# Regrouping the small matmuls of a chunked recurrence and of attention scores on TensorE

## The chip, the core and the metric

The program runs on one core of a Trainium2 chip. The metric is device time in microseconds (us) for one execution, as the median of the runs shown. TensorE has two clock levels, 1.2 and 2.4 GHz; the profile shows which share of the full level was granted in a stretch.

## What is computed

One decoder block on 512 tokens of width 1024, all in fp32. The parts that matter here are the RWKV-7 recurrence (12 heads of 64) and the scores of the dilated attention (12 heads of 64 in three groups):

```python
def step(state, inp):
    r_t, w_t, k_t, v_t, kk_t, a_t = inp
    sa = -jnp.einsum('bhvk,bhk->bhv', state, kk_t)
    state = (state * w_t[:, :, None, :]
             + sa[..., None] * (kk_t * a_t)[:, :, None, :]
             + v_t[..., None] * k_t[:, :, None, :])
    y = jnp.einsum('bhvk,bhk->bhv', state, r_t)
    return state, y
...
s = jnp.einsum('bhrnqd,bhrnkd->bhrnqk', qb, kc, preferred_element_type=jnp.float32)
s = s * (HEAD_DIM ** -0.5)
```

Around them stand the input projection (1024 to 6912 columns), the output projections and a SwiGLU of width 2816.

## The kernel before, in words

Every large product is made of three fp32r matmuls (high by high, high by low, low by high), each 128x128 by 128x512. Those of the input projection carry the names hh, hl, hi and lo; this text calls one of them a **filler**, since the scheduler sets them between the small matmuls. A small fp32 matmul leaves two records in the trace, here called **passes**.

The recurrence is cut into 8 chunks of 64 tokens (`c`), and runs for two groups of three head pairs: `rwkv_group(0)` and `rwkv_group(1)`. A pair is two heads, `e` = 0 and 1, that lie on partitions 0 to 63 and 64 to 127. In each group, after vectors are prepared (lines 413 to 512) and a forward substitution runs on VectorE (lines 515 to 530), come:

- the **block inverses** (lines 539 to 557): for each pair, 16 products `T` (`ps<-T,Sg`, 32 by 32, line 543) into one bank, copies of the result into `Q` by both engines, 16 products `Q` (`ps<-N,Q`, line 554) into one bank, and copies into `N`. In both, the 8 chunks of one head come first, then those of the other.
- the **chunk loop** (lines 565 to 619). Each chunk has a chain: six products `px` (`ps<-UV,Sg`, line 571), a scaling on ScalarE into `xs` (line 573), six products with `N` (`ps<-xs,N`, line 578), copies to `UV` on both engines (line 580), six products `h` (`ps<-UV,BK`, line 587), two VectorE operations on `H` (lines 593 and 594), and copies of `H` to `UV` (lines 595 and 596), which the next chunk reads.
- the **output products** (lines 598 to 609), after each odd chunk, for it and the chunk ahead of it. For each head one bank `py` is filled: a product with the state (`ps<-H,AR`, 64 by 64 of the array, line 607; none for chunk 0) and one with `UV` (`ps<-UV,Sg`, 128 by 64 of the array, line 608) by turns, pair after pair. ScalarE then copies the bank to `yb`. In a group these are 42 products of the first kind and 48 of the second.

The attention scores (lines 705 to 731) are made head by head: for each of four heads, 12 products `ps<-k,q` on 64 partitions, 128 or 256 columns wide, then a masked scaling and maxima on VectorE.

The order on each engine is set by a list scheduler that keeps dependencies, with priorities: `rwkv_group` runs under `tc.high_priority(PRI)`, so fillers of the sequences in `SEQ` are set where the chain would leave TensorE empty. PSUM has banks under four tags: three `mm`, two `b`, two `c`, one `y`. The program's order is fixed when it is built; nothing is reordered by the program at run time.

Of the kernel before, what the change touches and what calls it, by code (L numbers as in the profile page):

```python
# [18 lines left out]
P = 128  # L19
D = 1024  # L20
S = 512
KT = D // P
NTT = S // P
HD = 64
NPAIR = 6
GP = 3
NCH = 8
C = 64
# [25 lines left out]
A_M0 = 0  # L54
# [30 lines left out]
def block_kernel(ctx, tc, x, vec, cst, cst2, cst3, crow, ada, win0, lora, wts, wa, out):  # L85
    nc = tc.nc
    V, A, G = nc.vector, nc.scalar, nc.gpsimd
# [19 lines left out]
    def mm(o, l, r, start, stop):  # L107
        return nc.tensor.matmul(o, l, r, start=start, stop=stop)  # L108
# [159 lines left out]
    with ExitStack() as ph0:  # L268
# [83 lines left out]
        t = tmp("tg", 3)[:, 0:S]  # L352
# [7 lines left out]
        t = tmp("tg", 3)[:, 0:S]  # L360
# [37 lines left out]
    def rwkv_group(gi):  # L398
# [139 lines left out]
            G.memset(N[64 * e + 32:64 * e + 64, 0:32, :], 0.0)  # L538
        for p in range(GP):
            pq = bank("c")  # L540
            for e in range(2):
                for c in range(NCH):
                    mm(pq[64 * e + 32:64 * e + 64, c * 32:(c + 1) * 32], Sg[p][0:32, e, c, 32:64], t1a[:, e, :, p * NCH + c], True, True)
            qs = rp.tile([P, NCH * 32], F32, tag="xs", name=nm("Q"), bufs=2).rearrange("p (c t) -> p c t", t=32)
            pqv = pq[:, 0:256].rearrange("p (c t) -> p c t", c=NCH)
            A.copy(qs[32:64], pqv[32:64])
            V.tensor_copy(qs[96:128], pqv[96:128])
            for e in range(2):
                (A.copy, V.tensor_copy)[XE[e]](Sg[p][0:64, e, :, 0:C], AR[p][64 * e:64 * e + 64, :, 0:C])
            pn = bank("c")  # L550
            for e in range(2):
                hi32 = slice(64 * e + 32, 64 * e + 64)
                for c in range(NCH):
                    mm(pn[64 * e:64 * e + 32, c * 32:(c + 1) * 32], qs[hi32, c, :], N[hi32, 32:64, p * NCH + c], True, True)
            pnv = pn[:, 0:256].rearrange("p (c t) -> p c t", c=NCH)
            A.copy(N[0:32, 32:64, p * NCH:(p + 1) * NCH], pnv[0:32].rearrange("p c t -> p t c"))
            V.tensor_copy(N[64:96, 32:64, p * NCH:(p + 1) * NCH], pnv[64:96].rearrange("p c t -> p t c"))


        yb = rp.tile([P, GP, NTT, 2, HD], F32, tag="yb", name=nm("yb"))  # L560
# [4 lines left out]
        for c in range(NCH):  # L565
            px = bank("c")
            pxv = px[:, 0:GP * HD].rearrange("p (a v) -> p a v", a=GP)
            for p in range(GP):
                for e in range(2):
                    rows = slice(64 * e, 64 * e + 64)  # L570
                    mm(pxv[rows, p, :], Sg[p][:, e, c, 0:C], UV[:, c, e, p, :], True, True)
            xs = rp.tile([P, NCH * 32], F32, tag="xs", name=nm("xs"), bufs=2)[:, 0:GP * HD].rearrange("p (a v) -> p a v", a=GP)
            A.activation(xs, pxv, AF.Copy, scale=-1.0)
            pus = [bank("c"), bank("c")]
            for p in range(GP):
                for e in range(2):
                    rows = slice(64 * e, 64 * e + 64)
                    last_mm[0] = mm(pus[e][rows, p * HD:(p + 1) * HD], N[rows, :, p * NCH + c], xs[rows, p, :], True, True)
            for e in range(2):
                (V.tensor_copy if e else A.copy)(UV[0:64, c, e, :, :], pus[e][64 * e:64 * e + 64, 0:GP * HD].rearrange("p (a v) -> p a v", a=GP))  # L580
            if c < NCH - 1:
                ph = bank("c")
                phv = ph[:, 0:GP * HD].rearrange("p (a v) -> p a v", a=GP)
                for p in range(GP):
                    for e in range(2):
                        rows = slice(64 * e, 64 * e + 64)
                        mm(phv[rows, p, :], BN[p][:, c, rows], UV[:, c, e, p, :], True, True)
                Hn = rp.tile([P, GP, HD], F32, tag="H", name=nm("H"), bufs=3)
                db = dg[:, c, :, None].to_broadcast([P, GP, HD])
                if c == 0:  # L590
                    V.tensor_tensor(out=Hn, in0=phv, in1=db, op=ALU.mult)
                else:
                    V.tensor_tensor(out=Hn, in0=H, in1=phv, op=ALU.add)
                    V.tensor_tensor(out=Hn, in0=Hn, in1=db, op=ALU.mult)
                V.tensor_copy(UV[0:64, c + 1, 0], Hn[0:64])
                A.copy(UV[0:64, c + 1, 1], Hn[64:128])
            Hs.append(H)
            if c % 2 == 1:
                for e in range(2):
                    rows = slice(64 * e, 64 * e + 64)  # L600
# [8 lines left out]
                    A.copy(yb[:, :, c // 2, e, :], py[:, 0:GP * HD].rearrange("p (a v) -> p a v", a=GP))  # L609
# [95 lines left out]
    Ss = []  # L705
    for j in range(4):
        hp, e = j // 2, j % 2
        rows = slice(64 * e, 64 * e + 64)
        sb = ap_.tile([P, 1920], F32, tag="S", name=nm("S"), bufs=4)
        Ss.append(sb)  # L710
        q, k = qT[0][hp][rows], kT[0][hp][rows]
        b0, b1 = bank("b"), bank("c")
        mm(b0[:, 0:128], q[:, 0:128], k[:, 0:128], True, True)
        mm(b0[:, 128:384], q[:, 128:256], k[:, 0:256], True, True)
        mm(b1[:, 0:256], q[:, 256:384], k[:, 128:384], True, True)
        mm(b1[:, 256:512], q[:, 384:512], k[:, 256:512], True, True)
        V.scalar_tensor_tensor(out=sb[:, 0:384], in0=b0[:, 0:384], scalar=0.125, in1=cs3[:, A_M0:A_M0 + 384], op0=ALU.mult, op1=ALU.add)
        V.scalar_tensor_tensor(out=sb[:, 384:896].rearrange("p (a b) -> p a b", a=2), in0=b1.rearrange("p (a b) -> p a b", a=2), scalar=0.125,
                               in1=cs3[:, None, A_M0 + 128:A_M0 + 384].to_broadcast([P, 2, 256]), op0=ALU.mult, op1=ALU.add)
        for g in (1, 2):  # L720
            q, k = qT[g][hp][rows], kT[g][hp][rows]
            b = bank("b" if g == 1 else "c")
            for r in range(4):
                t = slice(r * P, (r + 1) * P)
                mm(b[:, t], q[:, t], k[:, t], True, True)
            mcol = A_M0 if g == 1 else A_M2
            V.scalar_tensor_tensor(out=sb[:, 384 + 512 * g:896 + 512 * g].rearrange("p (a b) -> p a b", a=4), in0=b.rearrange("p (a b) -> p a b", a=4), scalar=0.125,
                                   in1=cs3[:, None, mcol:mcol + P].to_broadcast([P, 4, P]), op0=ALU.mult, op1=ALU.add)
        V.tensor_reduce(out=mxs[:, 0:1, j], in_=sb[:, 0:128], axis=AX.X, op=ALU.max)
        V.tensor_reduce(out=mxs[:, 1:4, j], in_=sb[:, 128:896].rearrange("p (a b) -> p a b", a=3), axis=AX.X, op=ALU.max)  # L730
        V.tensor_reduce(out=mxs[:, 4:12, j], in_=sb[:, 896:1920].rearrange("p (a b) -> p a b", a=8), axis=AX.X, op=ALU.max)
    pr = [bank("b"), bank("b"), bank("c")]
    for g in range(3):
        for t in range(4):
# [119 lines left out]
    h2l = h2p.tile([P, KT, S], F32R, name="h2l")  # L854

    op_ = phO.enter_context(tc.tile_pool(name="op", bufs=1))
    ow = phO.enter_context(tc.tile_pool(name="ow", bufs=6))

    def natural_gemm(w0, nk, ah, al, tail, pool):
# [192 lines left out]
```

## Time and profile before

| | |
|---|---|
| runs shown | 1022.56, 1020.74, 1021.39 us, median 1021.39 |
| profiled execution | 1017.46 us, span 1015.7 us |
| granted clock, mean over the span | 0.984 |
| TensorE matmul busy | 982.6 us (97%) |
| VectorE busy | 580.0 us (57%) |
| ScalarE busy | 397.5 us (39%) |
| chain that ended last | TensorE 73%, VectorE 12%, issue 7%, DMA 6% |

Busy shares are averages over stages. A matmul counts as busy until its modelled end, so records overlap: how long a matmul holds the engine is read from the distance between starts. In the timeline a row merges records of one kind, and its duration runs from the first start to the last end.

### The profile page before, as it was taken

Reading aid. Unit: us, or ns where it says so; the run is one execution under the profiler, and the core shown is the slowest. Engines: PE = TensorE matmul, PEld = TensorE weight load, DVE = VectorE, ACT = ScalarE, POOL = GpSimd, SP = SyncE. Lnnn points to the kernel's source line nnn. Section 1 sums busy time; section 2 is a strip of 40 time slices with the busy share of each in tenths; the row PEclk is TensorE's granted clock in tenths of the full one; section 3 lists DMA queues with packets and bytes.
Section 4 is the critical chain, followed back from the end, with each engine's and each line's share of the span. In section 5 each row is a group of like instructions: output and inputs, shape, how many; then the busy total and the mean of one; then the engine's idle time right before and its main releaser. Section 6 shows DMA issues by size and latency. Waiting matters only on the chain.

```text
span 1015.7 us, 13832 instructions
## 1 busy us (share of the span) xinstructions
PE 982.6 (97%) x5468; PEld 781.7 (77%) x5468; DVE 580.0 (57%) x1050; ACT 397.5 (39%) x633; POOL 41.9 (4%) x85
## 2 busy tenths in 40 slices
PE   6999989999999999999999999999999999999997
PEld 4887767776767777677788878887888888888885
DVE  6985999634499984346645586755333333322234
ACT  7568453422366322222255245633233233222123
POOL 0000000100000010001000100010000000000000
PEclk9999999989999999989999999999999999999999
DMA  9653536312233232115634866063333323323322
GB/s 375 257 174 112 186 101 197 119 63 94 74 99 115 83 105 84 33 42 194 196 98 166 315 226 186 2 213 119 102 105 104 102 86 103 103 86 102 103 83 83
DMA packets 47170, 131.73 MB, mean 130 GB/s; under 512 B 11249, under 2 KB 12033, under 8 KB 47106
## 3 DMA queue, kind: packets, MB, share of 16 engines
q1 hardware_dynamic: 27792, 96.74, 29.2%
q10 hardware_dynamic: 13970, 16.27, 5.0%
q0 software_dynamic: 5344, 17.84, 4.8%
q8 instruction: 43, 0.70, 0.3%
q14 instruction: 21, 0.17, 0.1%
HBM read 116.14 MB, written 14.69 MB: 129 GB/s over the span
## 4 chain that ended last, share of the span: by engine, by line
PE 73%; DVE 12%; issue 7%; DMA 6%; ACT 1%; POOL 0%; ACTq 0%; DVEq 0%; POOLq 0%
PE ps L108 71%; DMA aw<-in_ada_dram 2%; DVE lo L112 2%; DVE fP L526 1%; DVE fT L530 1%; DMA d_ya<-t 1%; DVE Sg L486 1%; DVE aw L168 1%; DMA vc<-in_vec_dram 1%; DMA gb<-d_gate 1%; PE ps L308 1%; DMA t<-d_gate 1%; DMA k<-d_k 1%; ACT xg L490 0%; PE ps L910 0%
## 5 line engine op out<-in xcount | busy, mean ns | idle before, releaser
L111 ACT CAST hi<-raw 128x1024 fp32r<-128x1024 f32 (+1 forms) x130 | 133.2, 1025 | 367.5 <-PE ps L108 320.2
L112 DVE TENSOR_TENSOR lo<-raw,hi 128x1024 fp32r<-128x1024 f32 (+1 forms) x130 | 154.6, 1190 | 174.7 <-ACT hi L111 171.6
L108 PE MATMUL ps<-hh,lo 128*128 128x512 f32 x432 | 176.6, 409 | 0.6 <-DVE lo L112 0.6
L108 PE MATMUL ps<-hl,hi 128*128 128x512 f32 x432 | 176.5, 409 | 0.0
L108 PE MATMUL ps<-hh,hi 128*128 128x512 f32 x432 | 173.6, 411 | 1.0 <-ACT hi L111 0.7
L108 PE MATMUL ps<-h2h,hi 128*128 128x512 f32 (+1 forms) x352 | 133.6, 381 | 0.7 <-ACT u L940 0.7
L108 PE MATMUL ps<-h2h,lo 128*128 128x512 f32 (+1 forms) x352 | 133.4, 380 | 0.7 <-DVE lo L112 0.7
L108 PE MATMUL ps<-h2l,hi 128*128 128x512 f32 (+1 forms) x352 | 133.5, 381 | 0.0
L108 PEld LDWEIGHTS ps<-hh,hi 128*128 128x128 f32 x432 | 83.4, 193 | 19.9 <-issue 2.2
L108 PEld LDWEIGHTS ps<-hh,lo 128*128 128x128 f32 x432 | 83.3, 193 | 19.3 <-issue 1.1
L108 PEld LDWEIGHTS ps<-hl,hi 128*128 128x128 f32 x432 | 83.6, 194 | 17.8 <-issue 0.6
L108 PEld LDWEIGHTS ps<-h2h,lo 128*128 128x128 f32 x352 | 66.1, 188 | 13.6 <-DVE lo L112 1.1
L108 PEld LDWEIGHTS ps<-h2h,hi 128*128 128x128 f32 x352 | 66.0, 188 | 13.6 <-ACT u L940 0.9
L108 PEld LDWEIGHTS ps<-h2l,hi 128*128 128x128 f32 x352 | 66.1, 188 | 12.8
L168 DVE SCALAR_TENSOR_TENSOR aw<-aw,silur 128x1024 f32<-128x1024 f32 x48 | 58.3, 1220 | 8.3 <-DMA aw<-in_ada_dram 8.0
L941 DVE TENSOR_TENSOR u<-u,ps 128x512 f32<-128x512 f32 x22 | 15.0, 687 | 65.8 <-PE ps L108 58.5
L108 PE MATMUL ps<-lo,fh 128*128 128x512 f32 x144 | 44.4, 389 | 0.0
L108 PE MATMUL ps<-hi,fh 128*128 128x512 f32 x144 | 44.4, 389 | 0.0
L108 PE MATMUL ps<-hi,fl 128*128 128x512 f32 x144 | 44.3, 389 | 0.0
L108 PE MATMUL ps<-UV,Sg 128*64 128x64 f32 x384 | 40.3, 242 | 0.0
L108 PEld LDWEIGHTS ps<-UV,Sg 128*64 128x64 f32 x384 | 26.1, 141 | 10.5 <-issue 2.7
L108 PEld LDWEIGHTS ps<-hi,fh 128*128 128x128 f32 x144 | 27.0, 188 | 5.6
(292 smaller groups left out, 1426.3 us busy)
## 6 DMA issues: line engine op xcount, KB each, us to landing
raw<-in_wts_dram SPq DMA_DIRECT2D x124, 512.0 KB, 3.6
aw<-in_ada_dram SPq DMA_DIRECT2D x40, 512.0 KB, 3.7
d_gate<-t POOLq DMA_DIRECT2D x16, 256.0 KB, 3.4
aw<-in_ada_dram POOLq DMA_DIRECT2D x8, 512.0 KB, 4.6
raw<-in_win_dram SPq DMA_DIRECT2D x8, 384.0 KB, 6.8
raw<-in_wa_dram SPq DMA_DIRECT2D x8, 384.0 KB, 3.8
x<-in_x_dram SPq DMA_DIRECT2D x4, 512.0 KB, 5.4
t<-d_gate ACTq DMA_DIRECT2D x8, 256.0 KB, 4.3
```

Source lines behind the costliest of these rows:

```text
L108: return nc.tensor.matmul(o, l, r, start=start, stop=stop)
L111: A.copy(hi, src)
L112: V.tensor_tensor(out=lo, in0=src, in1=r32(hi), op=ALU.subtract)
L168: V.scalar_tensor_tensor(out=aw, in0=aw, scalar=1.0, in1=silur, op0=ALU.mult, op1=ALU.mult, accum_out=modv[:, i:i + 1])
L308: nc.tensor.transpose(pt[:, i * P:(i + 1) * P], xt[i][:, j * P:(j + 1) * P], ident)
L486: V.tensor_tensor(out=sgm[:, e, c0:c0 + 4, :], in0=pgr[e].rearrange("p (c t) -> p c t", c=4), in1=m_gram[:, None, :].to_broadcast([P, 4, 2 ...
L526: V.tensor_tensor(out=pv, in0=fU[:, t + 1 + a:t + 1 + b, t, None].to_broadcast([P, b - a, m]), in1=fT[:, t, None, 0:m].to_broadcast([P, b ...
L530: V.tensor_tensor(out=rows, in0=rows, in1=pv, op=ALU.add)
L941: V.tensor_tensor(out=u, in0=u, in1=pg, op=ALU.mult)
```

## The change

The two loops over chunk and head in the block inverses change places, so that the heads take turns. The `Q` products of the two heads go to two banks, `c` and `y`, in place of one. The output products take two banks at once, `y` and `b`: first all products with `H` for both heads and both chunks, then all with `UV`, and the flag that starts an accumulation is set only on the first write to a bank's half. The scores of the two heads of a pair are written by turns into a bank `b` and a bank `c`, and the four score tiles are allocated ahead. A pool gets an unused tile of 320 bytes per partition (`pad_o`), which moves addresses only.

```diff
         for p in range(GP):
             pq = bank("c")
-            for e in range(2):
-                for c in range(NCH):
+            for c in range(NCH):
+                for e in range(2):
                     mm(pq[64 * e + 32:64 * e + 64, c * 32:(c + 1) * 32], Sg[p][0:32, e, c, 32:64], t1a[:, e, :, p * NCH + c], True, True)
...
-            pn = bank("c")
-            for e in range(2):
-                hi32 = slice(64 * e + 32, 64 * e + 64)
-                for c in range(NCH):
-                    mm(pn[64 * e:64 * e + 32, c * 32:(c + 1) * 32], qs[hi32, c, :], N[hi32, 32:64, p * NCH + c], True, True)
...
+            pn = [bank("c"), bank("y")]
+            for c in range(NCH):
+                for e in range(2):
+                    hi32 = slice(64 * e + 32, 64 * e + 64)
+                    mm(pn[e][64 * e:64 * e + 32, c * 32:(c + 1) * 32], qs[hi32, c, :], N[hi32, 32:64, p * NCH + c], True, True)
...
             if c % 2 == 1:
+                py = [bank("y"), bank("b")]
+                tiles = [(p, par, e) for p in range(GP) for par in range(2) for e in range(2)]
+                for p, par, e in tiles:
+                    cc, rows = c - 1 + par, slice(64 * e, 64 * e + 64)
+                    if cc > 0:
+                        mm(py[e][64 * par:64 * par + 64, p * HD:(p + 1) * HD], AR[p][rows, cc, C:2 * C], Hs[cc][rows, p, :], p == 0, False)
+                for p, par, e in tiles:
+                    cc = c - 1 + par
+                    mm(py[e][64 * par:64 * par + 64, p * HD:(p + 1) * HD], Sg[p][:, e, cc, C:2 * C], UV[:, cc, e, p, :], cc == 0 and p == 0, p == GP - 1)
                 for e in range(2):
-                    rows = slice(64 * e, 64 * e + 64)
-                    py = bank("y")
-                    for par in range(2):
-                        cc = c - 1 + par
-                        for p in range(GP):
-                            o = py[64 * par:64 * par + 64, p * HD:(p + 1) * HD]
-                            if cc > 0:
-                                mm(o, AR[p][rows, cc, C:2 * C], Hs[cc][rows, p, :], True, False)
-                            mm(o, Sg[p][:, e, cc, C:2 * C], UV[:, cc, e, p, :], cc == 0, True)
...
+        def scores(g, cuts):
+            bs = [bank("b"), bank("c")]
+            for o, q, k in cuts:
+                for e in range(2):
+                    mm(bs[e][:, o], qT[g][hp][heads[e], q], kT[g][hp][heads[e], k], True, True)
+            return bs
```

The scheduler answers with another order. Three places on TensorE are shown; in a row, `x8` means eight equal matmuls that follow each other.

The block inverses of group 0, around the second pair, before:

```order
L108 MATMUL ps_2252<-hh,lo_2249 128x512
L108 MATMUL ps_2252<-hh,hi_2248 128x512
L108 MATMUL ps_1294<-N_1265,Q_1289 32x32 x8
L108 MATMUL ps_1313<-T_195_1264,Sg_889 32x32 x16
L108 MATMUL ps_2252<-hl,hi_2248 128x512
L108 MATMUL ps_2252<-hh,lo_2249 128x512
L108 MATMUL ps_2286<-hh,hi_2282 128x512
```

The same place in the change:

```order
L108 MATMUL ps_2255<-hh,hi_2251 128x512
L108 MATMUL ps_2255<-hl,hi_2251 128x512
L108 MATMUL ps_2255<-hh,lo_2252 128x512
L108 MATMUL ps_1314<-T_195_1264,Sg_889 32x32 x8
L108 MATMUL ps_1295<-N_1265,Q_1289 32x32 x8
L108 MATMUL ps_1314<-T_195_1264,Sg_889 32x32 x8
L108 MATMUL ps_2255<-hh,hi_2251 128x512
```

The 8 `Q` products of the first pair's second head and the 16 `T` products of the second pair are cut into three runs of 8, and fillers stand as they did. In the whole block inverses of group 0 the runs of small matmuls between fillers number 7 in place of 5, and 34 fillers in place of 32; in group 1 both have 6 runs, with 24 fillers in place of 35.

The output products of chunks 2 and 3 of group 0, before (`ps_1562` is the second head's bank; H and UV take turns):

```order
L108 MATMUL ps_1562<-H_1454,AR_918 64x64
L108 MATMUL ps_1562<-UV_874,Sg_879 64x64
L108 MATMUL ps_1562<-H_1454,AR_984 64x64
L108 MATMUL ps_1562<-UV_874,Sg_889 64x64
L108 MATMUL ps_1562<-H_1454,AR_1050 64x64
L108 MATMUL ps_1562<-UV_874,Sg_899 64x64
L108 MATMUL ps_1562<-H_1512,AR_918 64x64
L108 MATMUL ps_1562<-UV_874,Sg_879 64x64
L108 MATMUL ps_1562<-H_1512,AR_984 64x64
L108 MATMUL ps_1562<-UV_874,Sg_889 64x64
L108 MATMUL ps_1562<-H_1512,AR_1050 64x64
L108 MATMUL ps_1562<-UV_874,Sg_899 64x64
```

The same chunks in the change (`ps_1551` and `ps_1552` are the banks of the two heads):

```order
L108 MATMUL ps_1551<-H_1515,AR_984 64x64
L108 MATMUL ps_1552<-H_1515,AR_984 64x64
L108 MATMUL ps_1551<-H_1457,AR_1050 64x64
L108 MATMUL ps_1552<-H_1457,AR_1050 64x64
L108 MATMUL ps_1551<-H_1515,AR_1050 64x64
L108 MATMUL ps_1552<-H_1515,AR_1050 64x64
L108 MATMUL ps_1551<-UV_874,Sg_879 64x64
L108 MATMUL ps_1552<-UV_874,Sg_879 64x64
L108 MATMUL ps_2323<-hh,lo_2320 128x512
L108 MATMUL ps_2363<-hh,hi_2359 128x512
L108 MATMUL ps_1529<-xs_1527,N_1265 64x64
L108 MATMUL ps_1530<-xs_1527,N_1265 64x64
```

The products with `H` now follow each other, with the heads by turns, and the first two with `UV` stand ahead of the products with `N`; the ten others with `UV` come after those, five per head. Over a chunk loop the changes from one small kind of array tile to another fall from 71 to 14 in group 0 and from 70 to 17 in group 1, and the runs of small matmuls that begin after a filler from 35 to 30 and from 33 to 27. Fillers inside the loops: 87 before and 88 in the change in group 0, 64 and 65 in group 1. The three key-norm products of four small matmuls each that stood ahead of group 0's inverses stand in its chunk loop.

The scores, before (a bank of the second head, then one of the third):

```order
L108 MATMUL ps_4203<-k_4135,q_4129 128x128 x4
L108 MATMUL ps_4219<-k_4134,q_4128 128x128
L108 MATMUL ps_4219<-k_4134,q_4128 128x256
L108 MATMUL ps_4617<-hh,lo_4614 128x512
L108 MATMUL ps_4617<-hh,hi_4613 128x512
L108 MATMUL ps_4617<-hl,hi_4613 128x512
L108 MATMUL ps_4617<-hh,lo_4614 128x512
```

In the change, at the start of the first pair of heads:

```order
L108 MATMUL ps_4180<-k_4139,q_4133 128x128
L108 MATMUL ps_4181<-k_4139,q_4133 128x128
L108 MATMUL ps_4180<-k_4139,q_4133 128x256
L108 MATMUL ps_4181<-k_4139,q_4133 128x256
L108 MATMUL ps_4188<-k_4139,q_4133 128x256
L108 MATMUL ps_4189<-k_4139,q_4133 128x256
L108 MATMUL ps_4188<-k_4139,q_4133 128x256
L108 MATMUL ps_4189<-k_4139,q_4133 128x256
L108 MATMUL ps_4589<-hh,hi_4585 128x512
```

The heads take turns between two banks. The 48 score products stand in eight runs before, and in three in the change, of 8, 8 and 32; the last has no filler inside.

## Rows read from the trace of the kernel before

**Rows 1.** Page, busy us, share of the span, instructions, by engine.
```profile
PE 982.6 (97%) x5468; PEld 781.7 (77%) x5468; DVE 580.0 (57%) x1050; ACT 397.5 (39%) x633; POOL 41.9 (4%) x85
```

**Rows 2.** Windows, core 0: PE, PEld, DVE, ACT, POOL busy; clock; DMA share; GB/s.
```profile
184.40:205.30 20.90, 20.82 (x226) 16.55 (x226) 12.36 (x17) 9.13 (x15) 3.55 (x5) 0.84 0.34 114
205.30:272.10 66.80, 66.80 (x547) 45.57 (x546) 26.33 (x54) 19.42 (x45) 1.30 (x4) 0.95 0.25 80
272.10:368.40 96.30, 91.52 (x483) 71.07 (x481) 91.16 (x225) 50.31 (x74) 6.62 (x14) 1.00 0.31 103
368.40:389.70 21.30, 21.27 (x229) 17.08 (x229) 13.89 (x20) 6.57 (x12) 2.52 (x4) 0.92 0.32 102
389.70:450.20 60.50, 60.44 (x532) 41.73 (x531) 22.89 (x50) 16.94 (x41) 2.16 (x4) 0.98 0.15 45
...
480.50:513.40 32.90, 32.56 (x173) 24.42 (x173) 22.62 (x32) 6.85 (x10) 1.61 (x3) 0.95 0.62 200
```

**Rows 3.** Timeline, PE around a px burst: start, duration, line, operation, tiles, records.
```profile
222.42 0.40 PE L108 MATMUL ps<-hh,lo 128*128 128x512 f32 x1
...
222.75 0.57 PE L108 MATMUL ps<-UV,Sg 128*64 128x64 f32 x12
...
223.25 0.50 PE L108 MATMUL ps<-hh,hi 128*128 128x512 f32 x1
...
223.58 0.39 PE L108 MATMUL ps<-hl,hi 128*128 128x512 f32 x1
...
223.81 0.40 PE L108 MATMUL ps<-hh,lo 128*128 128x512 f32 x1
```

**Rows 4.** Timeline, PE: first of 12 alternating output products, and what follows.
```profile
235.28 0.33 PE L108 MATMUL ps<-H,AR 64*64 64x64 f32 x2
...
238.36 0.50 PE L108 MATMUL ps<-hl,hi 128*128 128x512 f32 x1
```

**Rows 5.** Timeline, PE: eight corner products of one head, and what follows.
```profile
184.49 1.07 PE L108 MATMUL ps<-T,Sg 32*32 32x32 f32 x16 [0.51 <-DVE T L534]
185.48 0.50 PE L108 MATMUL ps<-hl,hi 128*128 128x512 f32 x1
```

**Rows 6.** Timeline, PE at the lower clock: two fillers; a px burst, a filler.
```profile
195.71 0.63 PE L108 MATMUL ps<-hl,hi 128*128 128x512 f32 x1
196.13 0.63 PE L108 MATMUL ps<-hh,lo 128*128 128x512 f32 x1
...
205.28 0.91 PE L108 MATMUL ps<-UV,Sg 128*64 128x64 f32 x12
206.12 0.80 PE L108 MATMUL ps<-hh,hi 128*128 128x512 f32 x1
```

**Rows 7.** Timeline, all engines: one chunk of group 1, its chain from px.
```profile
426.10 0.57 PE L108 MATMUL ps<-UV,Sg 128*64 128x64 f32 x12
...
426.71 0.33 ACT L573 ACTIVATE xs<-ps 128x192 f32<-128x192 f32 x1 [1.86 <-PE ps L108]
...
427.26 0.88 PE L108 MATMUL ps<-xs,N 64*64 64x64 f32 x12
...
428.28 0.36 DVE L580 COPY UV<-ps 64x192 f32<-64x192 f32 x1 [3.52 <-PE ps L108]
...
428.73 0.57 PE L108 MATMUL ps<-UV,BK 128*64 128x64 f32 x12
...
430.69 0.35 ACT L596 COPY UV<-H 64x192 f32<-64x192 f32 x1
```

**Rows 8.** Timeline, VectorE in a chunk of group 0: one split.
```profile
230.93 1.23 DVE L112 TENSOR_TENSOR lo<-raw,hi 128x1024 fp32r<-128x1024 f32 x1 [1.86 <-ACT hi L111]
```

**Rows 9.** Timeline, scores: PE bursts and the row after, one reduction on DVE.
```profile
489.66 1.48 PE L108 MATMUL ps<-k,q 64*128 64x128 f32 x12
491.06 0.49 PE L108 MATMUL ps<-hl,hi 128*128 128x512 f32 x1
...
502.70 1.21 DVE L731 TENSOR_REDUCE mxs<-S 128x8 f32<-128x1024 f32 x1
```

More of the change, by code (lines that the diff above doesn't have):

```diff
@@ L549, in rwkv_group @@
                 (A.copy, V.tensor_copy)[XE[e]](Sg[p][0:64, e, :, 0:C], AR[p][64 * e:64 * e + 64, :, 0:C])
-            pn = bank("c")
-            for e in range(2):
-                hi32 = slice(64 * e + 32, 64 * e + 64)
-                for c in range(NCH):
-                    mm(pn[64 * e:64 * e + 32, c * 32:(c + 1) * 32], qs[hi32, c, :], N[hi32, 32:64, p * NCH + c], True, True)
-            pnv = pn[:, 0:256].rearrange("p (c t) -> p c t", c=NCH)
-            A.copy(N[0:32, 32:64, p * NCH:(p + 1) * NCH], pnv[0:32].rearrange("p c t -> p t c"))
-            V.tensor_copy(N[64:96, 32:64, p * NCH:(p + 1) * NCH], pnv[64:96].rearrange("p c t -> p t c"))
+            pn = [bank("c"), bank("y")]
[3 more added lines that the diff above has]
+                    mm(pn[e][64 * e:64 * e + 32, c * 32:(c + 1) * 32], qs[hi32, c, :], N[hi32, 32:64, p * NCH + c], True, True)
+            pnv = [b[:, 0:256].rearrange("p (c t) -> p t c", c=NCH) for b in pn]
+            A.copy(N[0:32, 32:64, p * NCH:(p + 1) * NCH], pnv[0][0:32])
+            V.tensor_copy(N[64:96, 32:64, p * NCH:(p + 1) * NCH], pnv[1][64:96])
         yb = rp.tile([P, GP, NTT, 2, HD], F32, tag="yb", name=nm("yb"))
@@ L598, in rwkv_group @@
             if c % 2 == 1:
-                for e in range(2):
-                    rows = slice(64 * e, 64 * e + 64)
-                    py = bank("y")
-                    for par in range(2):
-                        cc = c - 1 + par
-                        for p in range(GP):
-                            o = py[64 * par:64 * par + 64, p * HD:(p + 1) * HD]
-                            if cc > 0:
-                                mm(o, AR[p][rows, cc, C:2 * C], Hs[cc][rows, p, :], True, False)
-                            mm(o, Sg[p][:, e, cc, C:2 * C], UV[:, cc, e, p, :], cc == 0, True)
-                    A.copy(yb[:, :, c // 2, e, :], py[:, 0:GP * HD].rearrange("p (a v) -> p a v", a=GP))
+                py = [bank("y"), bank("b")]
[7 more added lines that the diff above has]
+                    mm(py[e][64 * par:64 * par + 64, p * HD:(p + 1) * HD], Sg[p][:, e, cc, C:2 * C], UV[:, cc, e, p, :], cc == 0 and p == 0, p == GP - 1)
+                for e in range(2):
+                    A.copy(yb[:, :, c // 2, e, :], py[e][:, 0:GP * HD].rearrange("p (a v) -> p a v", a=GP))
                 i = c // 2
@@ L704, in block_kernel @@
     mxs = ap_.tile([P, 12, 4], F32, name="mxs")
[L705 to L719, printed above, removed]
-        for g in (1, 2):
[L721 to L725, printed above, removed]
-            mcol = A_M0 if g == 1 else A_M2
[L727 to L731, printed above, removed]
@@ new lines, in block_kernel, with cut @@
+    Ss = [ap_.tile([P, 1920], F32, tag="S", name=nm("S"), bufs=4) for _ in range(4)]
+    for hp in range(2):
+        js = (2 * hp, 2 * hp + 1)
+        heads = [slice(0, 64), slice(64, 128)]
+        def scores(g, cuts):
[4 more added lines that the diff above has]
+            return bs
+        def cut(a, b):
+            return slice(a * P, b * P)
+        for e, b0 in enumerate(scores(0, [(cut(0, 1), cut(0, 1), cut(0, 1)), (cut(1, 3), cut(1, 2), cut(0, 2))])):
+            V.scalar_tensor_tensor(out=Ss[js[e]][:, 0:384], in0=b0[:, 0:384], scalar=0.125, in1=cs3[:, A_M0:A_M0 + 384], op0=ALU.mult, op1=ALU.add)
+        for e, b1 in enumerate(scores(0, [(cut(0, 2), cut(2, 3), cut(1, 3)), (cut(2, 4), cut(3, 4), cut(2, 4))])):
+            V.scalar_tensor_tensor(out=Ss[js[e]][:, 384:896].rearrange("p (a b) -> p a b", a=2), in0=b1.rearrange("p (a b) -> p a b", a=2), scalar=0.125,
+                                   in1=cs3[:, None, A_M0 + 128:A_M0 + 384].to_broadcast([P, 2, 256]), op0=ALU.mult, op1=ALU.add)
+        for g in (1, 2):
+            mcol = A_M0 if g == 1 else A_M2
+            for e, b in enumerate(scores(g, [(cut(r, r + 1),) * 3 for r in range(4)])):
+                V.scalar_tensor_tensor(out=Ss[js[e]][:, 384 + 512 * g:896 + 512 * g].rearrange("p (a b) -> p a b", a=4), in0=b.rearrange("p (a b) -> p a b", a=4), scalar=0.125,
+                                       in1=cs3[:, None, mcol:mcol + P].to_broadcast([P, 4, P]), op0=ALU.mult, op1=ALU.add)
+        for j in js:
+            sb = Ss[j]
+            V.tensor_reduce(out=mxs[:, 0:1, j], in_=sb[:, 0:128], axis=AX.X, op=ALU.max)
+            V.tensor_reduce(out=mxs[:, 1:4, j], in_=sb[:, 128:896].rearrange("p (a b) -> p a b", a=3), axis=AX.X, op=ALU.max)
+            V.tensor_reduce(out=mxs[:, 4:12, j], in_=sb[:, 896:1920].rearrange("p (a b) -> p a b", a=8), axis=AX.X, op=ALU.max)
@@ L856, in block_kernel @@
     op_ = phO.enter_context(tc.tile_pool(name="op", bufs=1))
+    op_.tile([P, 80], F32, name="pad_o")
     ow = phO.enter_context(tc.tile_pool(name="ow", bufs=6))
```

## The prediction

> **What bounds the kernel now.** The page's busy table comes first: TensorE is busy for 97% of the span and no other engine for more than 57% [rows 1]. That alone does not say that TensorE is the limit where the change acts, so the windows come next, cut at the stages [rows 2]. In the block inverses (184.4 to 205.3 and 368.4 to 389.7 us) and the chunk loops (205.3 to 272.1 and 389.7 to 450.2) TensorE is busy to the end, while VectorE works for 26.33 of 66.80 us and 22.89 of 60.50 us. Between the groups (272.1 to 368.4) it is the other way: VectorE is busy for 91.16 of 96.30 us. So time taken from TensorE in the four stages moves all that follows earlier; the stage between keeps its length, since VectorE sets it.
>
> The timeline then shows what a small matmul costs, by the distance of starts. A filler holds TensorE for 0.23 us (223.58 to 223.81). From the filler at 222.42 to the one at 223.58 are 1.16 us: two fillers, 0.46, and 0.70 for a px burst of 12 passes [rows 3]. Eight products of one head hold 1.00 us for 16 passes, of which I put 0.09 to leaving the run, so 0.057 a pass [rows 5]. px alternates the heads, whose results go to different columns of the array, and 12 passes one after the other would be 0.68 of its 0.70, with nothing left for entry and exit. I take it that two passes run side by side: 0.0285 each, 0.35 for the burst, and 0.35 for getting in and out of a run. The output products do worst: 12 of them, by turns with `H` and `UV`, go from 235.28 to 238.36, 0.257 each, where two passes alone would be 0.115 [rows 4]. A change of array tile thus costs about 0.14.
>
> **The change part by part.** *Block inverses.* 96 T and 96 Q products are 384 passes. Side by side each saves 0.0285, in all 10.9 us. Runs of small matmuls go from 11 to 13 over both groups, +0.7, and I leave 0.5 for passes that already overlap where one kind follows another: **-9.7 us**. The second group's inverses hold 11 fillers less; these come later and are neither gain nor loss. The copies of `Q` and `N` stay, and the second bank makes the next pair's Q products wait only for the copy of the pair before, a whole pair earlier.
>
> *Output products.* Now 84 products a group at 0.257 are two times 21.6 us, and the 6 others a group at 0.115 another 1.4: 44.6. After: 360 passes at 0.0285, 10.3; 31 changes of tile at 0.14, 4.4; and 11 runs fewer (68 to 57) at 0.35, a gain of 3.9. **-33.8 us**. No row shows `H` products of both heads next to each other, so this is bounded by the nearest rows: 0.057 if they queue [rows 5], 0.0285 as px [rows 3], and half of that if all four 64x64 tiles run at once, a further 2.4. px lies nearest for the UV products, which have its tile shape; I take it for both. The ScalarE copies of the two banks now stand together; ScalarE is busy for 19.42 of 66.80 us there [rows 2], so I cost them at nothing by themselves.
>
> *Scores.* A run of 12 passes holds 1.40 us (489.66 to 491.06) [rows 9]; 96 passes are at least eight times that, 11.2. Heads by turns halve it, -5.6, and 8 runs become 3, -1.75. But the last run has 32 products in five fills of two banks and no filler: its third fill waits until VectorE has emptied the first, and two maxima of 1.21 us stand in that queue [rows 9]. An estimate of 3.9 us of waiting leaves **-3.5 us**.
>
> *Clock.* The mean granted clock in the four stages is 0.84, 0.95, 0.92 and 0.98 [rows 2]; between levels of 1 and one half that is 6.7, 6.7, 3.4 and 2.4 us at 1.2 GHz, 19.2 in all. A filler then holds 0.42 in place of 0.23 (195.71 to 196.13), and the fall came after long stretches of small matmuls [rows 6]. If fillers fill half of the 19.2 us, 23 of them cost 4.4 us. With fewer us of small matmuls part of that should return; between nothing and 4.4 I take **-2 us**.
>
> *What is late next.* The chain of a chunk, from px to the copy of `H`, is 4.94 us (426.10 to 431.04) [rows 7]; eight are 39.5. Now a chunk takes 8.4 and 7.6 us on average. By the sums above the loops come to about 49 and 43 us, 6.1 and 5.4 a chunk: close to the chain. VectorE does other work in order among the chain's steps, such as a split of 1.23 us [rows 8], and what TensorE's output products hid until now will show in part. I put 0.4 us on each of 16 chunks and 1 us on each group's inverses: **+8 us**.
>
> *Nothing.* `pad_o` is no instruction. The key-norm products of the second group move behind the inverses; their user, the second group's preparation, begins after the loop. The weight DMAs stay in order, at a DMA share of 0.15 to 0.34 in the four stages [rows 2].
>
> Sum: -9.7 -33.8 -3.5 -2 +8 = **-41 us**, against the profiled execution of 1017.46 us (span 1015.7) 976.5. The median of the runs shown lies 3.9 above it, so I forecast **980 us**.
>
> **A rule that speaks against it.** The px burst has both heads' weights on all 128 rows of the array, and its 12 passes still hold no more than 0.70 us with entry and exit [rows 3]. The Trainium skill, "TensorE: Matmul & The Clock Gate", Part 3, says that a weight load overlaps running matmuls only when it targets another group of rows. By that, px could not overlap, nor could T and the UV products, which read the same rows for both heads; the time would be that of the first rival below. The trace as read here speaks against it, but the reading of px rests on how I split 0.70.
>
> **The rivals.**
> 1. *Only products on different rows run side by side.* Q, the `H` products and the scores gain, T (192 passes) and the UV output products (192) stay at 0.057: 384 times 0.0285 is 10.9 less gain, **991 us**. For it: no row shows T's heads by turns. Against it: px. Chance 0.12.
> 2. *The chain becomes the bound of the loops.* With the split and one more operation of its length in the way of each chunk, a chunk takes 4.9 + 2.4 = 7.3 us [rows 7, 8], 16 chunks 117 in place of 127.3 now. The loops give 10 in place of the 29 that I count (33.8 and about 1 of the clock, less 6.4): **999 us**. For it: the chunk is within 1.2 us of the chain already by my sum. Against it: VectorE is idle for 60% of the loops now. Chance 0.19.
> 3. *The clock.* If waits empty TensorE between denser bursts and it falls to 1.2 GHz through inverses and loops, the 211 fillers there (34, 88, 24, 65) cost 0.19 more each, 40 us, and 16 px bursts 0.84 in place of 0.50 [rows 6], 5.4; with the 2 us not returned, 980 + 47 = **1027 us**, slower than before. It decides once nine tenths of both stretches run at the lower level. Against it: 205.3 to 272.1 had a mean clock of 0.95 with long runs of output products. Chance 0.05.
>
> That the change does not do what it says I leave out: the order on TensorE shows the heads by turns at all three places.
>
> **How the numbers follow.** The forecast has 0.64. Its own range is 967 (no waits, -8; the rest of the clock, -2.4; four tiles at once, -2.4) to 990 (twice the waits, no clock gain). With the first rival and about half of the second, the range that should hold the time 8 times in 10 is 966 to 1000. Rival 3 is the case of slower, 0.05; 0.01 is left within 0.2%, which is about what a measurement of this kernel can tell from no change; faster 0.94.
>
> **What would show it.** In the profile after, T and Q should hold about 0.5 us per 8 products of each head and not 1.0, with the two heads' records interleaved; the output products of an odd chunk about 1.5 us and not 5 to 6; the two loops about 52 to 54 and 45 to 47 us. Busy TensorE time should fall by some 40 us, with idle gaps of tenths of a us in the chunk loops, released by VectorE's and ScalarE's copies, and some us in the long run of scores, released by VectorE's emptying of the score banks. The stage between the groups should last 96 us as now. The forecast is wrong if products in turn keep 0.057 a pass, if chunks take over 7 us with TensorE waiting for VectorE, or if the loops' granted clock falls below 0.9.

## The result, and the profile after

The change takes 990.28 us (median of 987.35, 990.25, 990.31 and 1000.87), the kernel before 1021.97 beside it: a ratio of 0.971, 95% interval 0.963 to 0.978. The profiled execution took 990.31 us (span 988.5), 27.2 us less than that of before. The prediction of 980 us was 10 too low; its range of 966 to 1000 holds the time, its forecast's own range (967 to 990) only just does not. Executions in a second, slower state are left out of every time and ratio here.

The first fence is the page's busy line after, the second its windows, cut from the first matmul of one stage to the first of the next: block inverses, loop, between the groups, inverses, loop; then the scores and the attention stage (from the maxima's products to the first output projection, `ps<-hi,mh`). They answer to [rows 1, 2].

```profile
PE 945.8 (96%) x5468; PEld 757.5 (77%) x5468; DVE 577.2 (58%) x1050; ACT 396.1 (40%) x633; POOL 41.9 (4%) x85
```

```profile
186.48:204.82 18.34, 17.95 (x227) 13.70 (x227) 11.96 (x15) 7.52 (x14) 3.00 (x4) 1.00 0.34 116
204.82:257.49 52.67, 52.67 (x573) 37.66 (x571) 26.18 (x58) 21.97 (x48) 1.18 (x3) 1.00 0.29 94
257.49:354.04 96.55, 91.63 (x481) 72.04 (x479) 90.84 (x226) 50.55 (x75) 7.36 (x17) 0.98 0.32 109
354.04:372.61 18.57, 17.98 (x216) 13.44 (x217) 11.02 (x15) 6.56 (x12) 1.90 (x3) 0.70 0.17 49
372.61:420.42 47.81, 47.81 (x527) 33.16 (x525) 21.75 (x49) 14.38 (x39) 1.62 (x3) 0.90 0.19 61
451.69:486.45 34.76, 31.19 (x186) 24.55 (x186) 24.66 (x36) 8.52 (x12) 2.15 (x4) 0.90 0.68 207
486.45:568.63 82.18, 77.71 (x424) 64.13 (x424) 41.62 (x50) 36.53 (x68) 6.47 (x12) 1.00 0.57 193
```

The same two last stages in the kernel before:

```profile
480.51:516.20 35.69, 35.32 (x184) 26.38 (x184) 25.23 (x35) 7.90 (x11) 2.15 (x4) 0.95 0.63 199
516.20:594.60 78.40, 78.09 (x426) 66.05 (x426) 42.30 (x50) 37.14 (x69) 6.48 (x12) 0.98 0.59 205
```

By stage, from first start to first start: inverses -2.5 and -2.7 us, loops -14.2 and -12.7, scores -0.9, but attention **+3.8**. The stretch up to the first inverse, which the change does not touch, is 2.0 longer, from the loop's end to the scores 0.9 longer, the rest within 1.2. That makes the 27.2.

The timeline of TensorE after shows the small matmuls. A burst of T, then one of Q, each with the filler behind it; then the output products of two chunks, with ScalarE's scaling `xs` among them:

```profile
188.50 1.14 PE L108 MATMUL ps<-T,Sg 32*32 32x32 f32 x30 [0.39 <-DVE T L534]
189.56 0.50 PE L108 MATMUL ps<-hh,hi 128*128 128x512 f32 x1
...
191.83 1.07 PE L108 MATMUL ps<-N,Q 32*32 32x32 f32 x16
192.83 0.50 PE L108 MATMUL ps<-hh,hi 128*128 128x512 f32 x1
...
250.57 0.34 PE L108 MATMUL ps<-H,AR 64*64 64x64 f32 x8
250.84 0.57 PE L108 MATMUL ps<-UV,Sg 128*64 128x64 f32 x12
251.34 0.45 PE L108 MATMUL ps<-H,AR 64*64 64x64 f32 x12
251.46 0.33 ACT L573 ACTIVATE xs<-ps 128x192 f32<-128x192 f32 x1 [0.20 <-PE ps L108]
251.72 0.45 PE L108 MATMUL ps<-UV,Sg 128*64 128x64 f32 x4
252.09 0.50 PE L108 MATMUL ps<-hh,lo 128*128 128x512 f32 x1
...
254.92 0.56 PE L108 MATMUL ps<-UV,Sg 128*64 128x64 f32 x10
255.41 0.50 PE L108 MATMUL ps<-lg_h,g_h 128*128 128x512 f32 x1
```

T holds 1.06 us for 30 passes, where 16 held 1.00 [rows 5]. Q still holds 1.00 for 16: nothing gained. The 12 passes of UV from 250.84 are the px burst of the last chunk: `xs`, which reads its result, starts just behind it, at 251.46. The 24 output products of this pair of chunks stand in six runs: H with 4, 8 and 12 passes (0.26, 0.27 and 0.38 us), UV with 4 from 251.72 (0.37) and 10 for each head (0.49 each, the first from 254.92). Together they hold 2.27 us, with the change of tile or the exit behind each run; by turns, 12 held 3.08 [rows 4], so 24 some 6.2.

To compare kernels, the distance from each record's start to the next start on TensorE is summed by kind over both groups (us; px is in the column of UV, in the change with 8.6 us, by the 12 passes ahead of each `xs`; stretches at the lower clock are in it):

| kernel | T | Q | H | UV, px | xs,N |
|---|---|---|---|---|---|
| before | 10.26 | 10.24 | 21.86 | 32.44 | 13.78 |
| the change | 6.80 | 10.32 | 7.07 | 19.01 | 13.44 |
| outputs only | | | 6.91 | 18.97 | |
| outputs, head by head | | | 9.06 | 19.28 | |
| outputs, no pairing | | | 10.46 | 21.90 | |
| outputs, kinds by turns | | | 13.62 | 27.10 | |
| Q by turns | 7.00 | 4.87 | 6.91 | 17.66 | 13.02 |
| Q by turns, flat N | 6.84 | 3.14 | 6.91 | 17.64 | 8.02 |

### The profile page after: what moved, and what is told of

It reads as the page before. It is cut to its first block, busy times and chain, and to the rows that moved or that the text cites. A ratio compares the mean times of both kernels' runs of the same rounds, so it can differ in the third digit from the quotient of the medians.

```text
span 988.5 us, 13834 instructions
## 1 busy us (share of the span) xinstructions
PE 945.8 (96%) x5468; PEld 757.5 (77%) x5468; DVE 577.2 (58%) x1050; ACT 396.1 (40%) x633; POOL 41.9 (4%) x85
## 4 chain that ended last, share of the span: by engine, by line
PE 74%; DVE 10%; issue 8%; DMA 5%; ACT 2%; ACTq 1%; POOL 0%; SPq 0%; DVEq 0%; POOLq 0%
PE ps L108 72%; DVE lo L112 1%; DVE fP L526 1%; DMA k<-d_k 1%; DVE fT L530 1%; DMA d_ya<-t 1%; DMA aw<-in_ada_dram 1%; DVE T L534 1%; DMA x<-in_x_dram 1%; DMA gb<-d_gate 1%; ACT xg L490 1%; DVE aw L168 1%; PE ps L308 1%; DVE Sg L486 0%; DMA VN<-d_v 0%
## 5 line engine op out<-in xcount | busy, mean ns | idle before, releaser
L108 PE MATMUL ps<-hh,lo 128*128 128x512 f32 x432 | 174.3, 403 | 0.8 <-DVE lo L112 0.8
L108 PEld LDWEIGHTS ps<-hh,hi 128*128 128x128 f32 x432 | 82.6, 191 | 18.6 <-issue 1.3
L108 PEld LDWEIGHTS ps<-hi,fl 128*128 128x128 f32 x144 | 27.0, 188 | 5.6
L108 PEld LDWEIGHTS ps<-lo,fh 128*128 128x128 f32 x144 | 27.0, 188 | 5.6
```

## The experiments

**The three parts alone.** Each kernel takes one part of the change's diff and leaves the rest as before.

```diff
+ block inverses of the change          (first kernel)
+ output products of the change         (second kernel)
+ scores of the change, with pad_o      (third kernel)
```

Inverses:

> The kernel before with only the block inverses of the change (T by turns, Q in two banks). As predicted (T and Q both side by side): T and Q together hold about 11 us less over both groups, the time falls by 9 to 10 us, to about 1012. By what the trace after shows (the scheduler still sets Q head by head, because the second head's copy ends later): T holds 3.5 us less (10.3 to 6.8), Q stays at 10.2 within 0.4, the time falls by 2 to 4 us, to 1017 to 1019. If T's gain was only given to the fillers or the clock: no fall.

Measured: 0.997, interval 0.994 to 1.001 (1020.33 against 1025.21). T holds 6.81, and Q gains nothing: 11.15, 0.9 more than before. The predicted fall of 9 to 10 us did not come; 2 to 4 fit, though the interval also allows nothing.

Output products:

> The kernel before with only the output products of the change (two banks, all products with H ahead of all with UV, heads by turns). As predicted: 33.8 us less by count, less 6 us of waits, 993 to 995. By the trace after: products with H hold 7 us a group in place of 21.9 for both, products with UV and px together 19 in place of 32.4, so 28 us less, 993 less up to 3 us given back at the scores and in the attention stage by transfers: 993 to 997. The rival (chain bounds the loops): TensorE idle in the loops for over 10 us and a time over 1000.

Measured: 0.970, 0.964 to 0.976 (992.30). This part alone is as fast as the whole change. The loops take 54.1 and 45.5 us with TensorE busy throughout, so the chain does not bound them.

Scores:

> The kernel before with only the scores of the change (heads by turns into banks b and c). As predicted: 3.5 us less, 1018. By the trace after: the passes themselves fall from 14.3 to about 8.5 us, and waits for transfers of k and for VectorE's emptying of the banks take 4 to 5 us of that; between 0 and 2 us less, 1019 to 1021.

Measured: 1.000, 0.997 to 1.004 (1025.34 against 1025.21). The predicted 3.5 us did not come; 0 to 2 lie within the interval. The windows of scores and attention in this kernel:

```profile
486.03:518.99 32.96, 29.72 (x186) 23.40 (x186) 24.48 (x36) 8.68 (x12) 1.61 (x3) 0.95 0.71 219
518.99:604.61 85.62, 80.81 (x424) 66.39 (x424) 43.10 (x52) 36.94 (x69) 7.01 (x13) 0.96 0.57 189
```

The scores are 2.7 us shorter, the attention stage 7.2 longer, though nothing ahead of them had become faster. `pad_o` goes with the new scores in every kernel here and was not tried by itself.

**Q by turns.** The change, with each Q product issued behind the one ahead of it:

```diff
-            for c in range(NCH):
-                for e in range(2):
+            last = None
+            for c in range(NCH):
+                for e in (1, 0):
...
+                        with tc.issue_after(last.ins if hasattr(last, "ins") else last):
+                            last = mm(*args)
```

> The change, with the Q products forced to alternate between the heads (each issued behind the one ahead of it, second head first). If Q passes of two heads run side by side as T's do: Q holds about 5.2 us over both groups in place of 10.3, and the time falls by 3 to 5 us, to about 986. If Q's passes queue for a reason of their own (other rows, other columns, a strided operand): Q stays at 57 ns a pass, 10.3 us, and the time is 990 or a little more, since the first head now waits for the second's copy.

Measured: 0.961, 0.956 to 0.966 (983.26), 7 us under the change, where 3 to 5 were expected. The last burst of a group's Q, and the px burst behind it:

```profile
202.75 1.08 PE L108 MATMUL ps<-N,Q 32*32 32x32 f32 x32
203.76 0.57 PE L108 MATMUL ps<-UV,Sg 128*64 128x64 f32 x12
```

32 passes in 1.01 us, where 16 took 1.00. Q holds 4.87 in place of 10.32. The heads' Q products run side by side once they alternate. The 5.5 us of Q are not all of the 7: in the profile of this kernel the second group ran at a granted clock of 1.00 in inverses and loop, in that of the change at 0.70 and 0.90, and what the clock gave was not told apart.

In the change the heads do not alternate. There the eight products of the first head, from 191.83, stand behind ScalarE's copy of `Q` and ahead of the end of VectorE's, which the second head needs:

```profile
190.22 0.37 ACT L546 COPY Q<-ps 32x256 f32<-32x256 f32 x1
...
192.02 0.43 DVE L547 COPY Q<-ps 32x256 f32<-32x256 f32 x1
```

**Grouping or pairing.** Three kernels on the outputs-only kernel, differing in the order of the output products. First, one head's products ahead of the other's:

```diff
-tiles = [(p, par, e) for p in range(GP) for par in range(2) for e in range(2)]
+tiles = [(p, par, e) for e in range(2) for p in range(GP) for par in range(2)]
```

> Only the output products of the change (992.3), kinds apart as in the change, but one head's products ahead of the other's. If most of the gain is the change of array tile that falls away (0.14 us at each): the passes go from 0.0285 to 0.057 where heads no longer alternate, so products with H hold 5 us a group in place of 3.3, those with UV 2.7 more: 8 to 9 us more in all, 1000 to 1001. If most of the gain is that the heads run side by side: 1010 to 1020, products with H back over 8 us a group.

Measured: 0.973, 0.970 to 0.975 (995.10). H holds 9.06, but UV as much as before the edit. I had overlooked that `par`, the chunk, alternates in this order: the two chunks of one head go to different columns of the array and run side by side. With H the heads lie on different rows, so H loses two of its four tiles. With UV the two heads of a chunk write to the same columns (`64 * par`, whatever `e`) and differ by the bank alone: only its two chunks ever ran side by side, and this order keeps them so. So a second order, one tile at a time:

```diff
+tiles = [(p, par, e) for e in range(2) for par in range(2) for p in range(GP)]
```

> Only the output products, two banks, H ahead of UV, but one head and one chunk at a time, so that three products in a row use the same tile and nothing stands next to a product of another tile, save where a run of one tile ends. If running side by side is worth the half of a pass: products with H hold 5.3 us a group (84 passes at 0.057 and the changes) in place of 3.2 to 3.7, and products with UV with px 2.7 more than 9.5: 9 to 10 us over both groups, time 1001 to 1003. If the two chunks of one head were already what ran side by side in the run with one head at a time (995.1), this one must be well above 995; if grouping alone is the gain, it stays at 995.

Measured: 0.976, 0.973 to 0.980 (999.59).

```profile
240.71 0.73 PE L108 MATMUL ps<-H,AR 64*64 64x64 f32 x12
241.37 1.26 PE L108 MATMUL ps<-UV,Sg 128*64 128x64 f32 x24
```

12 passes of H now hold 0.66 us in place of 0.38. UV rises by 1.5 us a group and not by the expected 2.7, since not all of it had run side by side. Side by side is worth 7 us (992.3 to 999.6), and 6.5 in the table; the other 22 to 25 us of this part (from 999.6 to the 1021.97 or 1024.46 of before, by the run beside it) (21.9 in the table) are the changes of tile that fell away. Third, the opposite, heads paired but H and UV by turns:

```diff
+                        for e in range(2):
+                            mm(... AR[p][rows, cc, C:2 * C], Hs[cc][rows, p, :], ...)
+                        for e in range(2):
+                            mm(... Sg[p][:, e, cc, C:2 * C], UV[:, cc, e, p, :], ...)
```

> Only the output products, two banks and heads by turns, but H and UV products by turns again after each pair of heads (H, H, UV, UV). By 0.14 to 0.15 us a change of tile: two changes for four products in place of four, so products with H hold about 7 us a group and products with UV with px about 13: half of the gain of 28 us is lost, time 1004 to 1008. If the heads side by side are what counts: close to 992. If the change of tile hides behind a paired pass: 992 to 996.

Measured: 0.992, 0.988 to 0.995 (1013.75).

```profile
236.43 0.33 PE L108 MATMUL ps<-H,AR 64*64 64x64 f32 x4
236.69 0.45 PE L108 MATMUL ps<-UV,Sg 128*64 128x64 f32 x4
237.07 0.33 PE L108 MATMUL ps<-H,AR 64*64 64x64 f32 x4
```

Two products of H and two of UV hold 0.64 us, where four by turns held 1.03 [rows 4]. The four passes of H hold 0.26 of it, those of UV 0.38: two heads of H run side by side, two heads of UV, on the same columns, do not. The sums by kind came as expected, the time 6 us above it; in the profiled execution the first loop ran at a mean clock of 0.86.

**The attention stage.** In the change TensorE waits there five times for a split of weights, 3.4 us in all. The first fence has the three longest waits; the second is ScalarE ahead of the first of them, which makes the split and stands at the issue of gate rows:

```profile
546.47 0.50 PE L108 MATMUL ps<-zh,hi 128*128 128x512 f32 x1 [1.00 <-ACT hi L111]
547.96 0.50 PE L108 MATMUL ps<-zh,lo 128*128 128x512 f32 x1 [0.76 <-DVE lo L112]
556.80 0.50 PE L108 MATMUL ps<-zh,hi 128*128 128x512 f32 x1 [0.82 <-ACT hi L111]
```

```profile
539.49 6.00 ACTq L810 DMA_DIRECT2D t<-d_gate  x3
545.59 0.83 ACT L111 CAST hi<-raw 128x768 fp32r<-128x768 f32 x1 [7.94 <-DMA t<-d_gate]
```

Two remedies were tried on the kernel with Q by turns: three more buffers for these rows, and the scores of before.

```diff
-        ga = tmp("tg", 3)[:, 0:S]
+        ga = ap_.tile([P, S], F32, tag="ga", name=nm("t"), bufs=3) if ct % 2 else tmp("tg", 3)[:, 0:S]
```

> The kernel with Q by turns and the scores of the change (983.3), with three more buffers for the gate rows that the output projections read in the attention stage. There ScalarE's queue stood 6 to 8 us at the issue of such a row until a write from the same buffer had landed, and TensorE waited for the split behind it. If that wait is the loss: the attention stage goes from 84 to 79 us and the time to 978 to 979. If the transfers themselves are the limit there (DMA share 0.94): no change beyond 1 us.

Measured: 0.962, 0.959 to 0.965 (984.30), no gain. TensorE's longest wait from the scores' end on (total, times, longest), and VectorE ahead of it:

```profile
PE ps L108 <- DVE gb L857: 4.3, 1, 4.3
```

```profile
553.06 0.69 DVE L857 TENSOR_TENSOR gb<-gb,ps 128x512 f32<-128x512 f32 x1 [6.81 <-DMA gb<-d_gate]
```

The waits for the splits are gone, and one of 4.3 us stands a step later, where VectorE, and TensorE behind it, wait for the next step's gate rows (`gb`). The wait only moved. That the transfers as a whole are the limit there is what this suggests; it was not tried to take any away.

> The kernel with Q by turns (983.3), but with the scores of the kernel before. If the scores of the change cost more in the attention stage (from the maxima's products to the first output projection: 84 us there, 78.4 before) than they save at the scores: scores and attention together 114 to 115 us in place of 118.8, time 978 to 980. If that loss comes from transfers that the earlier start crowds, whatever the order of the scores: attention stays at 82 to 84 and the time at 983 to 985, with the 1 to 2 us that the scores saved lost.

Measured: 0.960, 0.956 to 0.963 (982.50), against 983.26: no difference that can be told. In the profile the two stages together take 117.2 us, against 118.8 with the new scores and the 114 to 115 of the first expectation.

**A flat N.** In the loop a pair of products with N held 0.110 us and every other pair 0.058. N lies with its elements 128 bytes apart. The first burst with N in the kernel with Q by turns:

```profile
204.92 0.92 PE L108 MATMUL ps<-xs,N 64*64 64x64 f32 x12
205.78 0.51 PE L108 MATMUL ps<-hl,hi 128*128 128x512 f32 x1
```

```diff
-        N = rp.tile([P, C, 32], F32, tag="N", name=nm("N"))
+        N = rp.tile([P, 32, C], F32, tag="N", name=nm("N"))
...
-    mm(pus[e][rows, p * HD:(p + 1) * HD], N[rows, :, p * NCH + c], xs[rows, p, :], True, True)
+    mm(pus[e][rows, p * HD:(p + 1) * HD], N[rows, p * NCH + c, :], xs[rows, p, :], True, True)
```

> The kernel with Q by turns (983.3), with N laid out so that a product of the chunk loop reads its 64 elements next to each other and not 128 bytes apart. In every trace so far such a pair of products holds 0.110 us, where pairs of the other products hold 0.058. If the stride is the reason: these products hold about 4.3 us a group in place of 6.5, 4 to 5 us less over both, time 978 to 979. If the stride costs nothing: 6.5 us as now and 983. The two transposes into N now write with a stride and may take longer on VectorE, once a group: up to 1 us back.

Measured: 0.950, 0.947 to 0.954 (**973.01**), the fastest, beside one other, and faster than both kernels of this case.

```profile
199.35 0.69 PE L108 MATMUL ps<-N,Q 32*32 32x32 f32 x32
199.98 0.57 PE L108 MATMUL ps<-UV,Sg 128*64 128x64 f32 x12
...
201.14 0.61 PE L108 MATMUL ps<-xs,N 64*64 64x64 f32 x12
201.68 0.50 PE L108 MATMUL ps<-hl,hi 128*128 128x512 f32 x1
```

The products with N hold 8.02 us in place of 13.02, as expected. What I had not expected: Q, which reads N too, goes from 1.01 to 0.63 us for 32 passes. Together 6.7 us; the time fell by 10, and what the other 3 are was not told apart. The two transposes into N take 1.97 and 1.95 us in place of 1.24 and 1.20.

> The same with the three more buffers for the gate rows, as a candidate for the best version. By the two terms, 4 to 5 us for the stride and about 2 for the wait in the attention stage: 976 to 978. If one of them is nothing, 978 to 982.

Measured: 0.954, 0.951 to 0.957 (976.03), 3 us more than without the buffers: they bring nothing here either.

> The kernel with Q by turns and the flat N (973.0), with the scores of the kernel before. Scores and attention there take 34.7 and 85.2 us. If the scores of the change cost in the attention stage what the runs with the old ones have not (79.6 and 80.3 us there, 35.7 and 36.9 at the scores): 3 to 4 us less, 969 to 970. If the loss comes from the earlier start alone: attention stays above 83 us and the time at 972 to 975.

Measured: 0.952, 0.948 to 0.955 (972.97): in the range of the second expectation, though the attention stage fell as in the first. Scores and attention, with the new scores (973.01) and with the old:

```profile
429.99:464.69 34.70, 31.36 (x185) 24.64 (x185) 24.66 (x36) 8.73 (x12) 1.61 (x3) 0.90 0.66 206
464.69:549.88 85.19, 80.64 (x424) 66.43 (x424) 41.62 (x50) 36.64 (x68) 7.01 (x13) 0.96 0.56 187
```

```profile
435.15:472.44 37.29, 36.91 (x184) 27.50 (x184) 25.22 (x35) 8.15 (x12) 2.16 (x4) 0.91 0.60 190
472.44:550.25 77.81, 76.91 (x426) 64.81 (x427) 41.80 (x49) 36.78 (x69) 6.49 (x12) 1.00 0.58 203
```

In these two profiles the old scores win 4.8 us. The time does not show it: the profiled execution with the old scores ran its first loop at a mean clock of 0.91 and needed 56.84 us for it, the other at 1.00 and 52.32. Whether that is chance or follows from the order stays open; by the times the scores of the change are neither gain nor loss.

## Why the prediction was right or wrong

The direction, the place of the gain and most of its size were right; of the 41 us that were forecast against the profiled execution, 27.2 came (31.7 by the medians). By its own terms:

- **Block inverses, -9.7: the step that failed.** "The order on TensorE shows the heads by turns at all three places" is not so for Q. The order that I quoted shows the second head's eight Q products as one row, and I read the loop in the code in place of it. T gave 3.5 us of its 5.5, Q none. What the missing half was worth, the kernel with Q by turns shows: Q from 10.32 to 4.87, the time from 990.3 to 983.3, part of which may be the clock.
- **Output products, -33.8: the grouping right, the pairing of UV wrong, the size too large.** H and UV fell by 14.8 and 13.4, in all 28.2. H came as forecast: 7.07 us, where 168 passes at 0.0285 and half of the 4.4 for changes of tile are 7.0. UV did not: "px lies nearest for the UV products, which have its tile shape" holds for the shape, but px sends its two heads to different columns and the output products with UV do not. Without px their 192 passes hold 10.4 us, where the same sum gives 7.7, and the 24 products of two chunks hold 2.27 us, not the 1.5 named as a sign. Nor do the 3.9 us for fewer runs show: the loops' fillers hold 49.5 us for 151 before and 49.4 for 153 after. At full clock a filler between fillers holds 0.23 us, one ahead of a run 0.32 and one behind it 0.34; this is 0.2 of the 0.35 a run, and the rest lies in the small matmuls, so within the 28.2. Against it stand two more fillers, and 11 fillers at 1.2 GHz in place of 7. The split is shown by the kernel without pairing: of some 30 us, 7 are two or more tiles side by side, the rest is grouping.
- **Scores, -3.5: too much.** The stage gave 0.9, and the part alone nothing. I had 3.9 us of waiting for VectorE's emptying of the banks; that wait was 1.6, but two waits for `k` from memory, of 0.62 and 1.26, were not in the sum, nor the 3.8 us in the attention stage:

```profile
458.63 1.16 PE L108 MATMUL ps<-k,q 64*128 64x128 f32 x16 [0.62 <-DMA k<-d_k]
...
465.95 3.64 PE L108 MATMUL ps<-k,q 64*128 64x128 f32 x32 [1.26 <-DMA k<-d_k]
471.17 4.37 PE L108 MATMUL ps<-k,q 64*128 64x128 f32 x32 [1.59 <-DVE S L722]
```

- **Clock, -2: nothing.** The granted clock of the four stages is now 1.00, 1.00, 0.70 and 0.90; between the two levels that is 0.3 x 2 x 18.6 + 0.1 x 2 x 47.8 = 20.7 us at 1.2 GHz, 19.2 before. It gathered in the second group, where it fell in a burst of T and Q:

```profile
361.24 0.91 PE L108 MATMUL ps<-T,Sg 32*32 32x32 f32 x21
362.08 0.80 PE L108 MATMUL ps<-hl,hi 128*128 128x512 f32 x1
362.67 0.63 PE L108 MATMUL ps<-hh,lo 128*128 128x512 f32 x1
```

- **Chain waits, +8: some 6 too many.** TensorE is busy for all of 52.67 and 47.81 us of the loops. From the first inverse to the end of the second loop its waits are few, and none of them in a loop: 3.4 us at the inverses' start (1.3 before, so the 2 forecast for the inverses came), the other two between the groups.

```profile
PE ps L108 <- DVE T L534: 3.4, 4, 1.6
PE ps L108 <- DVE BK L474: 2.6, 2, 2.1
PE ps L509 <- ACT BK L497: 1.4, 1, 1.4
```

- **Nothing.** The key-norm products were costed at nothing; 24 of them now hold 2.6 us in the first loop, where none stood. Without them that loop would be at 50.0. They moved there from ahead of the inverses, so they are no miss in the sum.

The misses close the account only roughly: 6.2 us in the inverses, 5.6 in the output products, 2.6 and 3.8 from the scores, 2 of the clock and 2 ahead of the first inverse, less the 6 of waits that did not come, are 16.2, where 13.8 are missing; the lower clock is in the sums by kind too, so some of it counts twice. Seen from TensorE, its busy time fell by 36.8 us of the 40 forecast, and its idle time rose by 9.6, of which 7.4 lie in the scores and the attention stage. It is luck that waits forecast too high made up for a part of the gains forecast too high.

Of the rivals, the first gives 991 us, nearest to the time, and is still wrong as a mechanism: T, which reads the same rows for both heads, does run side by side, and Q, on different rows, did not because it never took turns; the products with UV came half-way to its 0.057 a pass, by their columns and not by their rows. The Trainium skill, "TensorE: Matmul & The Clock Gate", Part 3, has weight loads overlap running matmuls only for another group of rows; by the T burst above, 0.035 a pass with entry and exit against 0.057 for a pass alone, and 30 weight loads of 0.10 us and more within 0.97 us, the trace does not agree. The chain (second rival) bounds nothing here. The clock (third) took one stage to 0.70 and not both stretches.

## What to carry to other kernels

Read the order that the scheduler gives, row by row, for each product that is to take turns; a loop with heads inside is no proof, since a list scheduler takes what is ready first. Then see which rows each product reads and which columns it writes: two products in different banks, but on the same rows and columns, do not run side by side. For small matmuls first group those of one array tile shape, which here was worth 22 to 25 us, then alternate tiles, worth 7, and lay out what they read without gaps, worth 6.7. After such a gain look at what stood behind it: here transfers and queues in the attention stage took back what the scores had won.

## What the runs showed of the hardware

- **Reading with a stride makes a small matmul up to twice as long.** A pair of passes of a product with N held 0.110 us strided and 0.058 flat. With 128 bytes between its elements, N made 12 passes of the loop hold 0.86 us and 32 passes of Q 1.01; flat, 0.54 and 0.63, with entry or exit in each. The weight load of a product with N took 200 ns strided and 135 flat. The Trainium skill, "SBUF — State Buffer", section "Door 1: The DMA port swizzle", says that an access pays when it leaves its line of 16 bytes, four fp32 elements; that agrees, since here each element stands on a line of its own. T reads `t1a` with a stride too; a flat one was not tried.
- **Four tiles run at once.** Eight H passes on four 64x64 tiles hold 0.27 us, of which the last, with the change of tile behind it, takes 0.15; one tile at a time, 12 passes hold 0.66.
- **Changing the shape of the tile costs about 0.14 us each way.** By turns a product held 0.257 us [rows 4], as 0.107 for the first pass and 0.150 for the second, where two passes alone hold 0.115. The Trainium skill, "TensorEngine Tiling (Array Packing)", Key Properties, says that a change of tiling mode drains the engine; that agrees with the 0.64 us for two products of H and two of UV, whose passes alone would be 0.12 and 0.23: two changes cost the other 0.29. T and Q, of one shape, are mixed freely: in the change, passes of T and of Q start by turns from 193.97 us on, where the program has them in runs.
